# Second attention of a two-block transformer kernel: the outputs of a pair of heads are issued one pair later than its scores and exponentials, and the stage's buffers are cut into smaller parts

## The chip, the core and the metric

The kernel runs on one NeuronCore of a Trainium2 chip. The metric is the device time of one execution in microseconds (us), the median of several runs. Engines: TensorE (PE in the rows; its weight loads are PEld), VectorE (DVE), ScalarE (ACT), GpSimd (POOL) and SyncE (SP, which here issues the DMAs). Each engine works through its own queue in order; semaphores tie the queues together.

## What is computed

All in float32; one sequence of 2048 positions, width 1024. A first block (a short-convolution mixer, then stick-breaking attention) is followed by a second block:

```
proj = h @ w_in                     # u_pool, g_pool, q, k, v, g_attn, qi, ki, wi
pool_out = pool_mixer(u_pool, w_pool) * silu(g_pool)   # means over 2, 4, 8, 16 positions
# attention, for each block of 128 queries, 8 heads that share 2 key heads:
score  = sum over 8 index heads of relu(qi . ki) * wi      # causal
sel    = top 256 keys of score, per query
p      = softmax(q . k over the keys in sel)
attn   = (p @ v) * silu(g_attn)
x      = x + gate * (concat(pool_out, attn) @ w_out)
```

## The kernel before, in words

Activations lie channels by positions, weights are split into a high and a low part, and a projection (`lin`) is three matmuls of 128x512 for each 128 rows of the contraction (L119 to L121 in `lin`). Every phase is a Python generator; `merge` interleaves two or three of them by weights, which gives the order of emission, and a scheduler then sets the final order of each engine's queue from that order, from priorities and from its own model of durations. So the order around the change is the scheduler's, and has to be looked up, not read from the source.

The part that matters here begins after the first attention:

- `phase_e2` makes the gates and the pooling of the second block: `lin`, then on DVE a chain of shifted additions into tiles `ws` (L820), a last scaling (L824), the split into high and low (`split`, L81 on ACT and L82 on DVE, tile `pp`), and in `finish` a matmul of `pp` with `w_pool` (`lin<-pp`).
- `phase_f` is the second attention in eight groups of two query blocks. In step i, three generators are merged: attention of group i (`f_attn`), the search for the selected keys of group i+1 (`f_search`, on DVE: counts at L972, on ACT by a sign at L974, the last values at L1017 and L1018, equal scores at L1038 to L1041, whose result are the `masks`), and the index scores of group i+2 (`f_score`: matmuls L874 and L875, relu on ACT at L877, sum on DVE at L884).
- `f_block` does the attention of one query block, for four pairs of heads. For each head: scores of up to 2048 keys in chunks of 512 (two matmuls, L1150 and L1151, into a PSUM tile `z`), masking and maximum on DVE (L1152, into the row `fe`), the largest maximum (L1159), the bias (L1163), one exponential over the whole row on ACT with its sum (L1164). Then the outputs of the same pair: transposes of `fe` (L1173), copies to SBUF on ACT (L1175), matmuls with the values into `o` (L1181). After four pairs: the reciprocal of the sums, a copy on POOL that spreads it (L1193), four matmuls that turn it (L1197), two multiplications (L1198, L1199) and a store.
- `phase_g` projects with `w_out` for a quarter of the positions; quarters 0 to 2 fill gaps of `phase_f`, quarter 3 comes last.

PSUM has two banks for `z`, shared by index scores and attention scores, two for the transposes `tp`, one for `o` and three for `lin`. The row tiles `fe` are four of up to 2048 elements, so two pairs.

Of the kernel before, what the change touches and what calls it, by code (L numbers as in the profile page):

```python
# [19 lines left out]
P = 128  # L20
# [48 lines left out]
class Build:  # L69
# [72 lines left out]
    def bcast(self, r, name, chunk=None):  # L142

        nc = self.nc
        rb = self.norm_tile(name)
        for c in range(HT // CH) if chunk is None else [chunk]:
            ps = self.bank()
            for i in range(CH // P):
                b = c * (CH // P) + i
                nc.tensor.matmul(  # L150
                    ps[:, i * P : (i + 1) * P], r[:, b : b + 1].to_broadcast([P, P]), self.ident, start=True, stop=True
                )
            nc.scalar.copy(rb[:, c * CH : (c + 1) * CH], ps)
        return rb if chunk is None else rb[:, chunk * CH : (chunk + 1) * CH]
# [42 lines left out]
    def setup(self):  # L197
        nc = self.nc
        self.fixed = self.cp.tile([P, 2 * CH + 4 * CH + 1960], F32, name="fixed")
        self.fixedr = self.cp.tile([P, (4 + 1) * D], F32R, name="fixedr")  # L200
# [50 lines left out]
        own = self.fixedr[:, 4 * D :].rearrange("p (s k m) -> p s k m", s=2, k=4)  # L251
        self.wp = self.load_w("w_pool", 4, 0, own=own, keep=False)
# [523 lines left out]
    def phase_e2(self, chunks, x):  # L776
# [19 lines left out]
        def finish(g, q, ph, pw, sg):  # L796
            pm = self.lin([[w[g]] for w in self.wp], ([ph], [pw]), 1, 0)
# [3 lines left out]
        late = None  # L801
        for g in range(4):
# [31 lines left out]
    def act_chunk(self, pool):  # L834
        t = [pool.tile([P, 2, CH], F32R, name=f"gx{k}", tag="gx", bufs=12) for k in range(NKB)]
# [285 lines left out]
    def f_attn(self, qbs):  # L1121
        for qb in qbs:
            yield from self.f_block(qb)

    def f_block(self, qb):
# [5 lines left out]
        sg = self.turn("fsg", 1)  # L1131
        self.dma(sg.rearrange("p (j n) -> p j n", j=4), self.sg2[h][:, :, qs])
        o = self.psum("o")
        den = self.small("den", 8)
        for p in range(4):
            kv = p // 2
            q = self.turn("fq", 2)
            for d in range(2):
                self.dma(q[d * 64 : (d + 1) * 64], self.q2s[h][:, 2 * p : 2 * p + 2, :, qs])
            pe = []  # L1140
            for a in range(2):
                hd = 2 * p + a
                mx = self.small("mx", 4)
                row = self.at.tile([P, -(-W // HT) * HT], F32, name="fe", tag="fe", bufs=4)
                for c in range(nch):
                    c0 = c * CH
                    m = min(CH, W - c0)
                    keys = self.k2t[c0 // HT][:, kv, c0 % HT : c0 % HT + m]
                    z = self.psum("z")
                    nc.tensor.matmul(z[:, :m], q[:, a, 0], keys, start=True, stop=False)  # L1150
                    nc.tensor.matmul(z[:, :m], q[:, a, 1], keys, start=False, stop=True)  # L1151
                    nc.vector.tensor_tensor_reduce(  # L1152
                        row[:, c0 : c0 + m], z[:, :m], mb[:, c0 : c0 + m], 1.0, NEG, ALU.subtract, ALU.max, mx[:, c : c + 1]
                    )
                    yield 0.43 * m / CH
                sc = self.rq[:, qb, hd : hd + 1]
                if nch > 1:
                    top = self.small("ftop", 1)
                    nc.vector.tensor_reduce(top, mx[:, :nch], mybir.AxisListType.X, ALU.max)  # L1159
                else:  # L1160
                    top = mx[:, 0:1]
                nbs = self.small("nbs", 1)
                nc.vector.scalar_tensor_tensor(nbs, top, -1.0, sc, ALU.mult, ALU.mult)  # L1163
                nc.scalar.activation(row[:, :W], row[:, :W], AF.Exp, bias=nbs, scale=sc, accum_out=den[:, hd : hd + 1])  # L1164
                pe.append(row)
            for c in range(nch):
                nb = min(4, qb + 1 - 4 * c)
                wts = []
                for a in range(2):
                    tp = self.psum("tp")  # L1170
                    for j in range(nb):
                        k0 = c * CH + j * P
                        nc.tensor.transpose(tp[:, j * P : (j + 1) * P], pe[a][:, k0 : k0 + P], self.ident)  # L1173
                    wt = self.turn("fwt", 3)
                    last = nc.scalar.copy(wt[:, : nb * P], tp[:, : nb * P])  # L1175
                    wts.append(wt)
                with self.burst(last) as first:
                    for j in range(nb):
                        for a in range(2):
                            first(  # L1180
                                nc.tensor.matmul(  # L1181
                                    o[a * 64 : (a + 1) * 64, p * P : (p + 1) * P],
                                    self.v2t[c // 2][:, 4 * (c % 2) + j, kv * 64 : (kv + 1) * 64],
# [263 lines left out]
```

## Time and profile before

| | |
|---|---|
| median of 3 runs | 3415.56 us (3414.56 to 3417.75) |
| the profiled execution's own time | 3404.53 us, its span 3402.8 us |
| mean granted clock of TensorE | 0.973 of full speed |
| busy in the span | PE 3193.5 us, DVE 2254.1, ACT 1482.5, POOL 488.1 |

The profiled execution is 11 us below the median of the timed runs; durations and waits come from it alone. A line of the engines' busy times is an average over stages with different limits: the second attention, which the change touches, lies between about 2100 and 3400 us, and its own rows are read by stretch.

### The profile page before, as it was taken

How to read it: one execution, taken by the hardware profiler on the slowest of the kernel's cores; microseconds unless marked ns; L12 is line 12 of the kernel's file. 1: busy time of each engine (PE TensorE's matmuls, PEld its weight loads, DVE VectorE, ACT ScalarE, POOL GpSimd, SP SyncE). 2: the span in 40 equal slices, each digit the busy share in tenths (PEclk: the TensorE clock that was granted, in tenths of full speed). 3: DMA queues.
4: the chain of work that ended last, by engine and by line, in shares of the span. 5: the costliest groups of instructions: out<-in, count | busy, mean ns of one | idle time of the engine just before them, and what ended most of it. 6: DMA issues, size and time to landing. Idle time of an engine off the chain costs nothing. (4 is left out here: it accounts for less than half of the span.)

```text
span 3402.8 us, 49280 instructions
## 1 busy us (share of the span) xinstructions
PE 3193.5 (94%) x17922; PEld 2544.7 (75%) x17922; DVE 2254.1 (66%) x4508; ACT 1482.5 (44%) x2666; POOL 488.1 (14%) x600
## 2 busy tenths in 40 slices
PE   8999999999999999988999998889996998879897
PEld 7888888888788777766788776668875776657675
DVE  5344644544444987789888687998648578888641
ACT  4111411122222544556555555563453465865561
POOL 0000010000200000052212113420200431102002
PEclk9999999999999999999999999899998999999999
DMA  3111442333454554574466444645522552124005
GB/s 107 47 50 50 152 158 80 131 113 128 143 164 146 155 156 143 164 236 115 140 188 178 140 129 132 200 150 171 180 90 99 173 174 78 45 69 155 25 27 178
DMA packets 371396, 438.72 MB, mean 129 GB/s; under 512 B 25664, under 2 KB 271936, under 8 KB 371136
## 3 DMA queue, kind: packets, MB, share of 16 engines
q1 hardware_dynamic: 371136, 435.39, 41.3%
q8 instruction: 146, 2.39, 0.3%
q14 instruction: 114, 0.93, 0.1%
HBM read 308.94 MB, written 124.78 MB: 127 GB/s over the span
## 5 line engine op out<-in xcount | busy, mean ns | idle before, releaser
L119 PE MATMUL lin<-act,fixedr 128*128 128x512 f32 x1488 | 598.0, 402 | 12.7 <-DVE x1r L599 6.2
L120 PE MATMUL lin<-act,fixedr 128*128 128x512 f32 x1488 | 596.0, 401 | 7.1 <-DVE act L620 5.2
L121 PE MATMUL lin<-act,fixedr 128*128 128x512 f32 x1488 | 593.0, 399 | 0.0
L104 ACT ACTIVATE fixedr<-fixed 128x512 fp32r<-128x512 f32 x295 | 186.7, 634 | 729.8 <-PE lin L120 259.7
L548 DVE TENSOR_TENSOR_SCAN crf<-crf 128x512 f32<-128x512 f32 (+3 forms) x320 | 360.2, 1132 | 73.7 <-ACT crf L545 71.1
L119 PEld LDWEIGHTS lin<-act,fixedr 128*128 128x128 f32 x1488 | 283.2, 190 | 78.5 <-DVE x1r L599 8.4
L120 PEld LDWEIGHTS lin<-act,fixedr 128*128 128x128 f32 x1488 | 282.4, 190 | 72.1 <-DVE act L620 8.9
L105 DVE TENSOR_TENSOR fixedr<-fixed,fixedr 128x512 fp32r<-128x512 f32 x295 | 202.1, 685 | 198.5 <-ACT fixedr L104 189.1
L121 PEld LDWEIGHTS lin<-act,fixedr 128*128 128x128 f32 x1488 | 282.3, 190 | 62.1 <-issue 0.2
L1152 DVE CUSTOM_DVE_ANT_0 fe<-z,masks 128x512 f32<-128x512 f32 (+3 forms) x320 | 187.0, 606 | 131.9 <-PE z L1151 74.2
L119 PE MATMUL z<-act,fixedr 128*128 128x512 f32 x584 | 231.0, 396 | 12.0 <-ACT fixedr L104 12.0
L557 ACT COPY crf<-tp 128x512 f32<-128x512 f32 (+3 forms) x320 | 165.1, 530 | 175.9 <-PE tp L555 156.9
L551 POOL TENSOR_TENSOR crf<-crf 128x1 f32<-128x1 f32 x192 | 96.4, 504 | 931.9 <-ACT crf L538 672.6
L121 PE MATMUL z<-act,fixedr 128*128 128x512 f32 x584 | 229.8, 394 | 0.0
L120 PE MATMUL z<-act,fixedr 128*128 128x512 f32 x584 | 229.7, 394 | 0.0
L1175 ACT COPY ff<-tp 128x512 f32<-128x512 f32 (+3 forms) x320 | 160.0, 521 | 152.4 <-PE tp L1173 76.1
L538 ACT ACTIVATE crf<-z 128x512 f32<-128x512 f32 (+3 forms) x320 | 175.4, 549 | 112.8 <-PE tp L555 83.1
L884 DVE SCALAR_TENSOR_TENSOR sc<-ff,fixed,sc 128x512 f32<-128x512 f32 (+3 forms) x266 | 179.2, 694 | 53.1 <-ACT ff L877 51.3
L1173 PE MATMUL tp<-fixed,fe 128*128 128x128 f32 x1088 | 182.9, 287 | 31.7 <-ACT fe L1164 28.9
L1164 ACT ACTIVATE fe<-fe,fixed 128x128 f32<-128x128 f32 (+15 forms) x128 | 165.8, 1295 | 98.3 <-DVE fixed L1163 97.8
L549 DVE TENSOR_TENSOR crf<-crf 128x511 f32<-128x511 f32 (+3 forms) x320 | 198.3, 624 | 10.5 <-DVE crf L548 0.5
L877 ACT ACTIVATE ff<-z 128x512 f32<-128x512 f32 (+3 forms) x304 | 157.7, 544 | 99.0 <-PE z L875 94.0
(343 smaller groups left out, 6527.8 us busy)
## 6 DMA issues: line engine op xcount, KB each, us to landing
fixed<-in_w_in_a_dram SPq DMA_DIRECT2D x128, 256.0 KB, 2.8
fixedr<-kept_w_out SPq DMA_DIRECT2D x64, 512.0 KB, 4.8
kept_w_in<-fixedr SPq DMA_DIRECT2D x46, 512.0 KB, 4.2
fixedr<-kept_w_in SPq DMA_DIRECT2D x46, 512.0 KB, 3.5
crr<-kst SPq DMA_DIRECT2D x80, 256.0 KB, 5.1
crr<-qst SPq DMA_DIRECT2D x64, 256.0 KB, 5.7
fixed<-x2d SPq DMA_DIRECT2D x64, 256.0 KB, 3.8
ffr<-q2s SPq DMA_DIRECT2D x128, 128.0 KB, 2.7
```

Of the source, the lines that this page charges most:

```text
L104: nc.scalar.activation(t[:, 0], raw, AF.Copy)
L105: nc.vector.tensor_tensor(t[:, 1], raw, t[:, 0].bitcast(F32), ALU.subtract)
L119: self.nc.tensor.matmul(ps[:, :n], whi[k], a, start=k == 0, stop=False)
L120: self.nc.tensor.matmul(ps[:, :n], whi[k], b, start=False, stop=False)
L121: self.nc.tensor.matmul(ps[:, :n], wlo[k], a, start=False, stop=k == nk - 1)
L538: nc.scalar.activation(s[:, :W], z[:, :W], AF.Sigmoid)
L548: nc.vector.tensor_tensor_scan(er, er, er, left, ALU.mult, ALU.min)
L549: nc.vector.tensor_tensor(s[:, : W - 1], s[:, : W - 1], e[:, 1:W], ALU.mult)
L884: nc.vector.scalar_tensor_tensor(sc[:, c0 : c0 + m], r[:, :m], w, sc[:, c0 : c0 + m], ALU.mult, ALU.add)
L1152: nc.vector.tensor_tensor_reduce(row[:, c0 : c0 + m], z[:, :m], mb[:, c0 : c0 + m], 1.0, NEG, ALU.subtract, ALU.max, mx[:, c : c + 1])
L1164: nc.scalar.activation(row[:, :W], row[:, :W], AF.Exp, bias=nbs, scale=sc, accum_out=den[:, hd : hd + 1])
L1173: nc.tensor.transpose(tp[:, j * P : (j + 1) * P], pe[a][:, k0 : k0 + P], self.ident)
```

## The change

`f_block` is divided. `f_weights` does scores, masking and exponentials of one pair; `f_outputs` does transposes, copies and output matmuls. `f_attn` calls `f_outputs` for the pair before (kept in `self.behind`), also across blocks and groups; the last group empties it. The rows `fe` become eight tiles of 1024 (the same memory), and an exponential is done for each 1024 keys, so blocks 8 to 15 have two exponentials and two partial sums per head. The reciprocal is no longer spread by POOL: eight matmuls with 64 columns of weights read it through a stride of zero. The activations' tiles are halves of the former ones, the tiles `gx` of `phase_g` are 8 in place of 12, the `w_pool` weights are loaded by `phase_e2` in place of the start, and two merging weights differ.

```
-    def f_attn(self, qbs):
+    def f_attn(self, qbs, last):
         for qb in qbs:
-            yield from self.f_block(qb)
+            self.outs[qb] = [None, None]
+            for p in range(4):
+                pe = yield from self.f_weights(qb, p)
+                if self.behind is not None:
+                    yield from self.f_outputs(*self.behind)
+                self.behind = qb, p, pe
+        if last:
+            yield from self.f_outputs(*self.behind)
+            self.behind = None
...
-                row = self.at.tile([P, -(-W // HT) * HT], F32, name="fe", tag="fe", bufs=4)
+            row = [self.at.tile([P, HT], F32, name="fe", tag="fe", bufs=8) for _ in range(0, W, HT)]
...
-                nc.scalar.activation(row[:, :W], row[:, :W], AF.Exp, bias=nbs, scale=sc, accum_out=den[:, hd : hd + 1])
+            for u, x in enumerate(row):
+                x = x[:, : min(HT, W - u * HT)]
+                nc.scalar.activation(x, x, AF.Exp, bias=nbs, scale=sc, accum_out=den[:, u, hd : hd + 1])
...
-        rr = self.turn("frr", 1)
-        nc.gpsimd.tensor_copy(rr.rearrange("p (a d) -> p a d", a=8), rd.unsqueeze(2).to_broadcast([P, 8, 64]))
-        bc = self.psum("z")
-        for p in range(4):
-            ps = slice(p * P, (p + 1) * P)
-            nc.tensor.matmul(bc[:, ps], rr[:, ps], self.ident, start=True, stop=True)
+            bc = self.psum("z")
+            for i in range(4):
+                ps = slice(i * P, (i + 1) * P)
+                for a in range(2):
+                    row = rd[:, 2 * i + a : 2 * i + a + 1].to_broadcast([P, 64])
+                    nc.tensor.matmul(bc[a * 64 : (a + 1) * 64, ps], row, self.ident, start=True, stop=True)
...
-        t = [pool.tile([P, 2, HT], F32R, name=f"act{i}", tag=f"{pool.name}x", bufs=8) for i in range(n)]
-        return [x[:, 0] for x in t], [x[:, 1] for x in t]
+        t = [pool.tile([P, HT], F32R, name=f"act{i}", tag=f"{pool.name}x", bufs=16) for i in range(2 * n)]
+        return t[::2], t[1::2]
...
-        t = [pool.tile([P, 2, CH], F32R, name=f"gx{k}", tag="gx", bufs=12) for k in range(NKB)]
+        t = [pool.tile([P, 2, CH], F32R, name=f"gx{k}", tag="gx", bufs=8) for k in range(NKB)]
...
-        self.wp = self.load_w("w_pool", 4, 0, own=own, keep=False)
...
+        wp = self.load_w("w_pool", 4, 0, own=self.wk.tile([P, 2, 4, P], F32R, name="wp", tag="wp", bufs=1))
...
-            merge((self.ahead(self.phase_c(1), 2000), 250), (de, 300))
+            merge((self.ahead(self.phase_c(1), 2000), 260), (de, 300))
...
-            merge((de, 300), (until(f, lambda: self.e2), 230))
+            merge((de, 300), (until(f, lambda: self.e2), 250))
```

Three places of the queues show what the scheduler made of it.

**DVE, end of the pooling against the selection of blocks 8 and 9.** Before, the last additions `ws` of one chunk (L820, L824, L82) stand between and behind the selection's last steps (L1038 to L1041, `masks`):

```order
L1039 SCALAR_TENSOR_TENSOR masks_15956<-masks_15956 128x1152
L1032 COPY_PREDICATED fixed_84<-fixed_84 128x2
L1040 SCALAR_TENSOR_TENSOR masks_15956<-masks_15956,fixed_84 128x1152
L1041 SCALAR_TENSOR_TENSOR masks_15956,fixed_84<-sc_18628,fixed_84,masks_15956 128x1152
L820 TENSOR_TENSOR ws_20194<-ws_20192 128x525
L1038 TENSOR_SCALAR masks_15956<-sc_18629,fixed_84 128x1280
L82 TENSOR_TENSOR gx1_20295<-fixed_84,gx1_20295 128x512
L820 TENSOR_TENSOR ws_20196<-ws_20194 128x521
L1039 SCALAR_TENSOR_TENSOR masks_15956<-masks_15956 128x1280
L820 TENSOR_TENSOR ws_20198<-ws_20196 128x513
```

After, the same chunk (L819, L823 there) stands among the steps of the search itself, which are short but for the counts (L971); the steps on equal scores (L1037 to L1040 there) come some 70 rows later:

```order
L819 TENSOR_TENSOR ws_20244<-ws_20242 128x525
L977 SCALAR_TENSOR_TENSOR fixed_84<-fixed_84 128x4
L984 SCALAR_TENSOR_TENSOR fixed_84<-fixed_84 128x2
L819 TENSOR_TENSOR ws_20246<-ws_20244 128x521
L979 COPY_PREDICATED fixed_84<-fixed_84 128x8
L986 RECIPROCAL fixed_84<-fixed_84 128x2
L819 TENSOR_TENSOR ws_20248<-ws_20246 128x513
L991 TENSOR_TENSOR fixed_84<-fixed_84 128x2
L987 TENSOR_TENSOR fixed_84<-fixed_84 128x2
L823 SCALAR_TENSOR_TENSOR ws_20248<-ws_20248,u_20180 128x512
```

So the pooling's chain no longer has the selection's long last steps ahead of it.

**PE, the last pair of block 8.** Before, the last scores of the pair's second head (`z_22174`) are followed after 22 instructions by the first transpose of that head's row (`fe_22165`):

```order
L1151 MATMUL z_22174<-keys_18565,ffr_15958 128x128
L874 MATMUL z_22201<-keys_18565,ffr_15958 128x256
L875 MATMUL z_22201<-keys_18565,ffr_15958 128x256
L1173 MATMUL tp_22105<-fixed_84,fe_21978 128x128
L1181 MATMUL o_21552<-ff_15957,keys_15903 64x128 x8
L1173 MATMUL tp_22181<-fixed_84,fe_22144 128x128 x4
L874 MATMUL z_22208<-keys_15903,ffr_15958 128x512
L875 MATMUL z_22208<-keys_15903,ffr_15958 128x512
L1181 MATMUL o_21552<-ff_15957,keys_18565 64x128 x2
L874 MATMUL z_22281<-keys_15903,ffr_15958 128x512
L875 MATMUL z_22281<-keys_15903,ffr_15958 128x512
L1173 MATMUL tp_22187<-fixed_84,fe_22165 128x128
```

After, the same scores (`z_22176`) stand here, with outputs of the pair before and projections of `phase_g` (`lin<-gx`) behind them:

```order
L1161 MATMUL z_22176<-keys_18619,ffr_16025 128x128
L1221 MATMUL o_21871<-ff_16024,keys_18619 64x128 x2
L1213 MATMUL tp_22229<-fixed_84,fe_22007 128x128 x4
L120 MATMUL lin_22317<-gx3_21758,fixedr_85 128x512
L873 MATMUL z_22180<-keys_18619,ffr_16025 128x256
L874 MATMUL z_22180<-keys_18619,ffr_16025 128x256
L121 MATMUL lin_22317<-gx3_21758,fixedr_85 128x512
```

and the first transpose of that head's row (`fe_22166`) stands here, 101 instructions behind those scores:

```order
L1161 MATMUL z_22367<-keys_15966,ffr_16025 128x512
L121 MATMUL lin_22460<-gx7_21762,fixedr_85 128x512
L119 MATMUL lin_22567<-gx0_21755,fixedr_85 128x512
L120 MATMUL lin_22567<-gx0_21755,fixedr_85 128x512
L121 MATMUL lin_22567<-gx0_21755,fixedr_85 128x512
L119 MATMUL lin_22567<-gx1_21756,fixedr_85 128x512
L1221 MATMUL o_21871<-ff_16024,keys_18619 64x128 x2
L1213 MATMUL tp_22400<-fixed_84,fe_22166 128x128 x4
```

What moved: the way from a row's scores to its transposes on PE is over four times as many instructions long here. In blocks 13 to 15, where scores of the next pair already stood ahead of outputs before, it grows less.

**PE, from block 9 to block 10.** Before, the last outputs of block 9 (`o_22311`) come ahead of 16 pairs of index scores and then the first scores of block 10; the end of that piece:

```order
L875 MATMUL z_23024<-keys_18565,ffr_15958 128x512
L874 MATMUL z_23029<-keys_18565,ffr_15958 128x256
L875 MATMUL z_23029<-keys_18565,ffr_15958 128x256
L1150 MATMUL z_23060<-keys_15903,ffr_15958 128x512
L1151 MATMUL z_23060<-keys_15903,ffr_15958 128x512
```

After, block 10's first two rows of scores (`z_23133` to `z_23185`) stand ahead of the normalizer (L1204) and of the last pair's transposes of block 9 (L1213):

```order
L1160 MATMUL z_23176<-keys_15966,ffr_16025 128x512
L1161 MATMUL z_23176<-keys_15966,ffr_16025 128x512
L873 MATMUL z_23180<-keys_15966,ffr_16025 128x512
L874 MATMUL z_23180<-keys_15966,ffr_16025 128x512
L1160 MATMUL z_23185<-keys_18619,ffr_16025 128x384
L1161 MATMUL z_23185<-keys_18619,ffr_16025 128x384
L1204 MATMUL z_23193<-fixed_84 64x128 x8
L873 MATMUL z_23223<-keys_18619,ffr_16025 128x512
L874 MATMUL z_23223<-keys_18619,ffr_16025 128x512
L873 MATMUL z_23248<-keys_18619,ffr_16025 128x384
L874 MATMUL z_23248<-keys_18619,ffr_16025 128x384
L1213 MATMUL tp_23339<-fixed_84,fe_23131 128x128 x4
```

So a block's last outputs now lie behind scores that need the next group's masks on DVE.

## Rows read from the trace of the kernel before

**Rows 1.** The page's first part: busy us, share of the span, instructions.

```profile
PE 3193.5 (94%) x17922; PEld 2544.7 (75%) x17922; DVE 2254.1 (66%) x4508; ACT 1482.5 (44%) x2666; POOL 488.1 (14%) x600
```

**Rows 2.** Windows: busy us by engine, granted clock, DMA share, GB/s.

```profile
2580.00:2611.00 31.00, 28.82 (x128) 22.96 (x126) 24.85 (x101) 14.72 (x21) 2.10 (x7) 1.00 0.43 147
2611.00:2640.00 29.00, 1.95 (x6) 1.29 (x5) 28.02 (x62) 4.83 (x10) 3.49 (x3) 0.52 0.03 9
2640.00:2783.00 143.00, 137.08 (x801) 108.07 (x800) 83.22 (x190) 72.43 (x131) 44.78 (x46) 0.95 0.53 170
2783.00:3177.00 394.00, 341.04 (x2262) 265.28 (x2262) 350.44 (x987) 239.01 (x404) 82.40 (x71) 0.95 0.28 90
2783.00:2864.00 81.00, 73.04 (x439) 57.86 (x439) 77.31 (x226) 42.89 (x74) 33.17 (x24) 0.96 0.39 127
2931.00:3037.00 106.00, 88.02 (x625) 66.11 (x624) 100.16 (x295) 77.44 (x124) 8.20 (x7) 0.93 0.12 33
3088.00:3177.00 89.00, 75.39 (x522) 59.58 (x521) 86.02 (x248) 44.32 (x65) 15.82 (x10) 0.95 0.28 95
3177.00:3332.00 155.00, 145.09 (x1259) 109.93 (x1258) 61.58 (x220) 95.71 (x142) 2.22 (x5) 0.99 0.08 23
```

**Rows 3.** Timeline of PE at 2638 us: start, us, instruction, idle before.

```profile
2638.42 0.79 PE L119 MATMUL lin<-pp,fixedr 128*128 128x512 f32 x1 [27.05 <-ACT pp L81]
2639.01 0.63 PE L119 MATMUL lin<-act,fixedr 128*128 128x512 f32 x1
...
2642.85 0.47 PE L119 MATMUL lin<-act,fixedr 128*128 128x512 f32 x1
...
2645.26 0.40 PE L120 MATMUL lin<-act,fixedr 128*128 128x512 f32 x1
```

**Rows 4.** Timeline of DVE in the same stretch.

```profile
2629.61 0.70 DVE L820 TENSOR_TENSOR ws<-ws 128x525 f32<-128x525 f32 x1
...
2632.24 2.81 DVE L1039 TENSOR_TENSOR_SCAN masks<-masks 128x1280 int16<-128x1280 int16 x1
...
2637.02 0.68 DVE L824 SCALAR_TENSOR_TENSOR ws<-ws,u 128x512 f32<-128x512 f32 x1
```

**Rows 5.** Waits of PE from 2783 to 3177: us in total, times, longest.

```profile
PE tp L1173 <- ACT fe L1164: 21.5, 9, 6.5
PE z L1150 <- DVE fixed L1152: 10.9, 5, 3.8
PE o L1181 <- ACT ff L1175: 6.6, 6, 2.0
...
PE z L1197 <- POOL ff L1193: 1.8, 2, 1.3
```

**Rows 6.** Timeline of all engines around 2855 us.

```profile
2854.10 1.68 DVE L1041 SCALAR_TENSOR_TENSOR masks<-sc,fixed,masks 128x1408 uint8<-128x1408 f32 x1
...
2855.70 0.15 DVE L1163 SCALAR_TENSOR_TENSOR fixed<-fixed 128x1 f32<-128x1 f32 x1
...
2857.38 0.90 PE L1173 MATMUL tp<-fixed,fe 128*128 128x128 f32 x3 [6.46 <-ACT fe L1164]
```

**Rows 7.** Groups by shape: busy us, mean ns of one.

```profile
L1164 ACT ACTIVATION_READ_ACCUMULATOR fe<-fe,fixed 128x1 f32 x128 | 24.2, 189 | 0.0
L1164 ACT ACTIVATE fe<-fe,fixed 128x2048 f32<-128x2048 f32 x8 | 16.8, 2099 | 5.2 <-DVE fixed L1163 5.2
L1164 ACT ACTIVATE fe<-fe,fixed 128x1024 f32<-128x1024 f32 x8 | 9.9, 1244 | 1.0 <-DVE fixed L1163 0.9
```

**Rows 8.** Timeline of PE in the last block.

```profile
3317.12 1.09 PE L1181 MATMUL o<-ff,keys 128*64 128x128 f32 x16 [1.48 <-ACT ff L1175]
...
3318.64 1.06 PE L1197 MATMUL z<-fixed,ff 128*128 128x128 f32 x8
```

**Rows 9.** Timeline of all engines around 2609 us.

```profile
2608.62 1.13 ACT L1164 ACTIVATE fe<-fe,fixed 128x896 f32<-128x896 f32 x1
...
2611.23 0.15 DVE L975 TENSOR_SCALAR fixed<-fixed 128x1 f32<-128x1 f32 x1 [2.45 <-ACT masks L974]
```

More of the change, by code (lines that the diff above doesn't have):

```diff
@@ L140, in rstd, with bcast @@
         return r
-    def bcast(self, r, name, chunk=None):
+    def bcast(self, r, name, chunk=None, into=None):
         nc = self.nc
-        rb = self.norm_tile(name)
+        rb = self.norm_tile(name) if into is None else into
         for c in range(HT // CH) if chunk is None else [chunk]:
@@ L1130, in f_block @@
         mb = self.masks[qb]
[L1131 to L1134, printed above, removed]
-        for p in range(4):
[L1136 to L1140, printed above, removed]
-            for a in range(2):
-                hd = 2 * p + a
-                mx = self.small("mx", 4)
-                row = self.at.tile([P, -(-W // HT) * HT], F32, name="fe", tag="fe", bufs=4)
[L1145 to L1163, printed above, removed]
-                nc.scalar.activation(row[:, :W], row[:, :W], AF.Exp, bias=nbs, scale=sc, accum_out=den[:, hd : hd + 1])
[L1165 to L1183, printed above, removed]
-                                    wts[a][:, j * P : (j + 1) * P],
-                                    start=(c == 0 and j == 0),
-                                    stop=(c == nch - 1 and j == nb - 1),
-                                )
-                            )
-                yield 0.44 * nb
@@ new lines, in f_weights, with f_outputs @@
+        if p == 3:
+            rd = self.small("rd", 8)
+            if W > HT:
+                nc.vector.tensor_tensor(rd, den[:, 0], den[:, 1], ALU.add)
+                nc.vector.reciprocal(rd, rd)
+            else:
+                nc.vector.reciprocal(rd, den[:, 0])
+            self.outs[qb][1] = rd
+        return pe
+    def f_outputs(self, qb, p, pe):
+        nc = self.nc
+        h, qs = qb // 8, slice(qb % 8 * P, qb % 8 * P + P)
+        nch = (qb * P + P + CH - 1) // CH
+        kv = p // 2
+        sg = self.gates[qb]
+        if p == 0:
+            self.outs[qb][0] = self.psum("o")
+        o, rd = self.outs[qb]
+        if p == 3:
+            bc = self.psum("z")
+            for i in range(4):
+                ps = slice(i * P, (i + 1) * P)
+                for a in range(2):
+                    row = rd[:, 2 * i + a : 2 * i + a + 1].to_broadcast([P, 64])
+                    nc.tensor.matmul(bc[a * 64 : (a + 1) * 64, ps], row, self.ident, start=True, stop=True)
+            nc.vector.tensor_tensor(sg, bc, sg, ALU.mult)
+        for c in range(nch):
+            nb = min(4, qb + 1 - 4 * c)
+            wts = []
+            for a in range(2):
+                tp = self.psum("tp")
+                for j in range(nb):
+                    k0 = c * CH + j * P
+                    nc.tensor.transpose(tp[:, j * P : (j + 1) * P], pe[a][k0 // HT][:, k0 % HT : k0 % HT + P], self.ident)
+                wt = self.turn("fwt", 3)
+                last = nc.scalar.copy(wt[:, : nb * P], tp[:, : nb * P])
+                wts.append(wt)
+            with self.burst(last) as first:
+                for j in range(nb):
+                    for a in range(2):
+                        first(
+                            nc.tensor.matmul(
+                                o[a * 64 : (a + 1) * 64, p * P : (p + 1) * P],
+                                self.v2t[c // 2][:, 4 * (c % 2) + j, kv * 64 : (kv + 1) * 64],
+                                wts[a][:, j * P : (j + 1) * P],
+                                start=(c == 0 and j == 0),
+                                stop=(c == nch - 1 and j == nb - 1),
+                            )
+                        )
+            yield 0.44 * nb
+        if p == 3:
+            nc.vector.tensor_tensor(sg, o, sg, ALU.mult)
+            self.dma(self.cata[h][:, :, qs], sg.rearrange("p (j n) -> p j n", j=4))
+            self.seen[qb] = self.small("seen", 1)
+            nc.gpsimd.tensor_copy(self.seen[qb], sg[:, 0:1])
+            self.attended += 1
+            yield 1.0
@@ L1230, in phase_f @@
             )
+        self.behind, self.outs, self.den, self.gates = None, {}, {}, {}
         for i in range(-2, len(groups)):
```

64 lines of the change are left out of this document (43 added, 21 removed).

## The prediction, made before the changed kernel ran

> **What bounds the kernel now.** I read the page's first part, then the second attention cut into windows, then PE's waits in the worst of these, then the timelines around the two largest. PE is busy 3193.5 of 3402.8 us [rows 1], so 209 us are all that could come back at unchanged PE work, and the change touches only waits that lie in the second attention. The windows [rows 2] show three kinds of stretch there. From 2611 to 2640 us PE does almost nothing (1.95 of 29 us) while DVE works 28.02: a hole with DVE as its cause. From 2783 to 3177 us PE works 341.0 and DVE 350.4 of 394: neither is full over the whole of it; in the three selections inside it (2783 to 2864, 2931 to 3037, 3088 to 3177) DVE has 263.5 of 276 us, so DVE bounds these, and PE bounds what lies between. From 3177 to 3332 us PE is at 145.1 of 155 and DVE at 61.6: PE bounds the last blocks. From 2640 to 2783 likewise (137.1 of 143).
>
> The hole is one wait of 27.05 us of the pooling's matmul for its input `pp` [rows 3]. DVE's timeline says why [rows 4]: the pooling's additions (L820, L824) stand among the selection's last steps for blocks 8 and 9, of which the scan L1039 alone takes 2.81 us. After the hole the first nine matmuls come at (2642.85 - 2639.01) / 9 = 0.427 us each, the next ten at (2645.26 - 2642.85) / 10 = 0.241 [rows 3]; the granted clock of the hole's window is 0.52 [rows 2], so the idle stretch also cost clock, of the two levels the one of 1.2 GHz.
>
> In the stretch from 2783 to 3177 us PE waits 21.5 us for exponentials, 10.9 for DVE to free a bank of scores, 6.6 for copies, 1.8 for the normalizer's copy on POOL [rows 5]. The longest of them, 6.46 us, is a chain in which ACT was not late by itself: DVE did L1041 of the selection for 1.68 us, then at 2855.70 the bias L1163, only then could ACT start, and PE's transposes came at 2857.38 [rows 6].
>
> **What the change does to each.**
>
> *The hole.* After the change the chunk's additions stand among the short search steps, ahead of the steps on equal scores. The wait of 27.05 us goes, and with it the slow matmuls, 9 x (0.427 - 0.241) = 1.7 us. What is late next: `pp` still needs its chain through DVE, whose search steps contain counts. I leave +6 us for the last chunks' small waits; the bounds are 0 (every chunk hidden behind its two projections of 24 matmuls, 48 x 0.241 = 11.6 us) and 27 (the wait only changes its place). I choose near the low end because in the order none of the 2 to 3 us steps stands inside the chain any more. Sum: -27.05 - 1.7 + 6 = -22.8.
>
> *The lag.* The transposes of a row come more than a hundred instructions after its scores where they came after 22, so the 6.46 us and its like should be covered. But a wait of PE that goes returns time only where DVE can also go on: in the selections DVE is idle 276 - 263.5 = 12.5 us, in the whole stretch 394 - 350.4 = 43.6. The bounds are therefore 0 and about -44 (the waits of [rows 5] add up to 40.8). I take -10, near the 12.5: the exponential waits lie mostly where DVE is full. From 3177 on, PE already runs nearly without gaps, so I count nothing there.
>
> *The normalizer.* POOL's copy goes, and with it PE's waits of 1.8 us [rows 5]. Four matmuls of 128 columns of weights become eight of 64. The old four take 1.06 us (8 records), and eight matmuls of the very new shape, the outputs, take 1.09 (16 records) [rows 8]: so 16 blocks x 0.03 = 0.5 us, nothing. Sum -1.8 + 0.5 = -1.3. The Trainium skill, "TensorE: Matmul & The Clock Gate", section "Back-to-back issue gap", prices a matmul by its moving columns alone; by that, eight with 128 moving columns would take twice the four, 1.06 x 16 = 17 us more. The trace's 1.09 against 1.06 us speaks against it here, where consecutive matmuls go to the two halves of the output partitions.
>
> *The split exponentials.* Blocks 8 to 15 have 64 rows wider than 1024, so 64 exponentials more. Two of 1024 and the extra read cost 2 x 1244 + 189 - 2099 = 578 ns more than one of 2048 [rows 7], 64 x 0.578 = 37 us of ACT. ACT is busy 239 of 394 and 95.7 of 155 us there [rows 2]; the cover is the lag itself, since PE does another pair's outputs meanwhile. If that cover is gone, a pair pays up to 0.58 us for each head. The Trainium skill, "VectorE: DVE Perf Modes", section "The TRN2 errata — SBUF-src ops pay a fixed extra latency per instruction", speaks against such splitting: small tiles pay the fixed part each. With its 224 cycles of ScalarE the estimate is 64 x 0.19 = 12 us; the rows here give three times that, since the read of the sum is paid as well.
>
> *The rest.* Loading `w_pool` in `phase_e2` adds one load, one split and one store for the first half and a load for the second, where the DMA engines are at 0.43 and less [rows 2]: 0. Halved activation tiles keep their bytes: 0. With eight `gx` tiles in place of twelve a quarter of `phase_g` can't load ahead; quarters 0 to 2 are filling, so 0, at worst some 5 us where a quarter follows directly. The merging weights move the beginnings of phases by little in the order: 0.
>
> *Sum:* -22.8 - 10 - 1.3 = -34.1 us against the profiled execution's 3404.5, which gives 3370.4, a ratio of 0.9900. The runs' median is 3415.56, so 3381.
>
> **The rivals.**
>
> 1. *Slower: ACT delays the search.* One of a selection's two counts runs on ACT (L974), and DVE waits for it at each of its eight steps; at 2611.23 DVE waited 2.45 us because an exponential of 1.13 us stood ahead [rows 9]. Now two heads' exponentials stand together, so a count may find a second row ahead of it: 2 x 1244 + 2 x 189 ns = 2.9 us. With three selections from 2783 on, 24 steps: at 2.0 us each DVE, already full, is 48 us longer; -22.8 - 1.3 + 48 = +24, 3439. It decides from 24 / 24 = 1.0 us a step on; from (24 + 7) / 24 = 1.3 it is slower by more than measurement can tell. Against it: ACT is busy 239 of 394 us only, and the scheduler can put the count first.
> 2. *Only the hole closes.* DVE sets the pace of the selections, and PE's waits for exponentials turn into waits for DVE's masks or for a bank of scores, since block 10's scores now stand ahead of block 9's last outputs. Then -22.8 - 1.3: 3380.4 profiled, 3391.5.
> 3. *The change doesn't do what it says:* the hole moves to a neighbouring chunk (the +6 becomes 27) and the lag returns only a few us: -2 to -8, some 3410.
> 4. *Everything comes back:* hole without a rest and all of DVE's idle time: -28.8 - 43.6 - 1.3 = -73.7, which is 3342. In favour: the clock of 0.95 in that stretch [rows 2] would rise with fewer gaps.
> 5. *The eight matmuls cost double,* as the skill's rule has it: 3381 + 17 = 3398. The mechanism in this kernel would be that the two halves don't overlap when the weights are read through a stride of zero.
>
> **How the numbers follow.** The forecast has a chance of 0.44 (3381, its own range 3366 to 3393), rival 2 0.18, rival 1 0.17, rival 4 0.10, rival 5 0.05, rival 3 0.06. A measurement of this kernel tells about 0.2%, 6.8 us, from no change, so the border is 3408.7. Of the four cases that gain, 0.77 together, I move 0.06 across it, for the uncertainty of a sum of this kind; so faster 0.71. Rival 1 spills 0.01 into the middle and keeps 0.16, and 0.02 of rival 3 turns slower: 0.18. The same: the rest, 0.11. The range for 8 in 10 runs from 3350 (leaving out half of rival 4) to 3428 (leaving out the greater part of rival 1): about 0.05 below and 0.13 above.
>
> **What the profile after would show.** Hole right: no PE wait above about 3 us for `pp`, and DVE's steps on equal scores behind the pooling's last split. Lag right: PE's waits for exponentials between the first selection and the last below 5 us in place of 21.5, and the stretch from block 10's selection to the last one shorter than 394 us. Lag useless: the same sum of PE waits there under another name (scores for DVE). ACT right: exponentials 192 in number, ACT's busy time some 37 us up, and DVE's waits for L974's counterpart not above the 2.45 us a step seen here. Normalizer: sixteen records in about 1.1 us. The prediction is wrong above all if DVE's selections get longer, or if a new wait of 20 us appears at another boundary of phases, since the scheduler reorders every queue.

## The result, and the profile after

The changed kernel takes 3372.81 us (median of 4 runs, 3368.09 to 3374.52) against 3415.91 us before (4 runs, 3414.56 to 3417.75): a ratio of 0.9871, 95% interval 0.9854 to 0.9888, or 43 us less. The forecast was 3381 with a range from 3350 to 3428. The profiled execution's span fell from 3402.8 to 3366.0 us.

The first part of the page after, which answers to [rows 1]:

```profile
PE 3213.1 (95%) x18050; PEld 2546.6 (76%) x18050; DVE 2244.8 (67%) x4516; ACT 1502.8 (45%) x2794; POOL 464.9 (14%) x584
```

PE's idle time went from 3402.8 - 3193.5 = 209.3 us to 3366.0 - 3213.1 = 152.9, 56.4 us less; but its busy time rose by 19.6 us, which the forecast did not have. The difference is the 36.8 us of the span.

The windows of the changed kernel, with the columns of [rows 2]: from just behind the pooling's end to the selection of blocks 10 and 11; from there to the end of the last selection; the three selections; the last blocks:

```profile
2640.00:2760.00 120.00, 114.36 (x722) 88.26 (x723) 77.27 (x178) 62.22 (x117) 31.26 (x25) 0.99 0.42 134
2760.00:3146.00 386.00, 352.39 (x2308) 265.52 (x2309) 350.54 (x990) 255.70 (x492) 73.34 (x73) 0.96 0.34 107
2760.00:2858.00 98.00, 96.69 (x589) 75.06 (x589) 91.79 (x265) 58.07 (x117) 33.47 (x32) 0.98 0.56 179
2909.00:3031.00 122.00, 107.17 (x775) 77.94 (x774) 114.25 (x319) 97.13 (x185) 9.20 (x7) 0.98 0.13 38
3041.00:3146.00 105.00, 96.46 (x593) 73.65 (x593) 95.73 (x262) 55.89 (x95) 23.79 (x25) 0.97 0.49 156
3146.00:3301.00 155.00, 148.06 (x1304) 110.88 (x1300) 64.84 (x228) 103.29 (x185) 0.79 (x5) 1.00 0.09 27
```

Against [rows 2] the stretch of the selections is 386 us long in place of 394, with the same DVE work (350.5 and 350.4) but 352.4 us of PE work in place of 341.0: PE's idle time in it fell from 53.0 to 33.6. Each selection by itself got longer (81 to 98, 106 to 122, 89 to 105 us), because more of DVE's other work now lies inside it: in the second, for example, 14 us more of the sums of index scores (L883). By the prediction that was the first sign of its being wrong; it came, and the kernel is faster all the same.

PE's longest waits in that stretch, which answer to [rows 5]:

```profile
PE z L1160 <- DVE fixed L1162: 7.2, 5, 1.8
PE z L1160 <- ACT ff L876: 6.3, 8, 2.1
PE z L873 <- ACT ff L876: 5.8, 5, 3.6
PE tp L1213 <- ACT fe L1176: 5.2, 6, 1.9
```

The wait for exponentials fell from 21.5 to 5.2 us. In its place stand waits of 12.1 us for a PSUM bank that ACT's relu (L876) has yet to read (in L1160 and L873): PE runs ahead of ACT and DVE now, where before it stood behind them.

The hole, on PE and then on DVE, answering to [rows 3] and [rows 4]:

```profile
2627.86 0.51 PE L119 MATMUL lin<-pp,wp 128*128 128x512 f32 x1 [3.14 <-ACT pp L81]
```

```profile
2624.63 0.68 DVE L823 SCALAR_TENSOR_TENSOR ws<-ws,u 128x512 f32<-128x512 f32 x1
...
2636.03 2.56 DVE L1038 TENSOR_TENSOR_SCAN masks<-masks 128x1152 int16<-128x1152 int16 x1
```

27.05 us became 3.14: the last scaling of the pooling (L823) now comes 11 us ahead of the first long step on equal scores (L1038).

### The profile page after: what moved, and what is told of

Same layout as the page of the kernel before. It is cut to its first block, busy times and chain, and to the rows that moved or that the text cites. A ratio compares the mean times of both kernels' runs of the same rounds, so it can differ in the third digit from the quotient of the medians.

```text
span 3366.0 us, 49652 instructions
## 1 busy us (share of the span) xinstructions
PE 3213.1 (95%) x18050; PEld 2546.6 (76%) x18050; DVE 2244.8 (67%) x4516; ACT 1502.8 (45%) x2794; POOL 464.9 (14%) x584
## 5 line engine op out<-in xcount | busy, mean ns | idle before, releaser
L1176 ACT ACTIVATE fe<-fe,fixed 128x1024 f32<-128x1024 f32 (+7 forms) x192 | 189.5, 991 | 74.2 <-DVE fixed L1173 73.6
L883 DVE SCALAR_TENSOR_TENSOR sc<-ff,fixed,sc 128x512 f32<-128x512 f32 (+3 forms) x266 | 177.7, 692 | 47.8 <-ACT ff L876 47.2
L1213 PE MATMUL tp<-fixed,fe 128*128 128x128 f32 x1088 | 189.8, 284 | 16.4 <-ACT fe L1176 11.5
L876 ACT ACTIVATE ff<-z 128x512 f32<-128x512 f32 (+3 forms) x304 | 156.9, 547 | 92.4 <-PE z L874 72.9
```

Source lines behind the costliest of these rows:

```text
L883: nc.vector.scalar_tensor_tensor(sc[:, c0 : c0 + m], r[:, :m], w, sc[:, c0 : c0 + m], ALU.mult, ALU.add)
L1176: nc.scalar.activation(x, x, AF.Exp, bias=nbs, scale=sc, accum_out=den[:, u, hd : hd + 1])
L1213: nc.tensor.transpose(tp[:, j * P : (j + 1) * P], pe[a][k0 // HT][:, k0 % HT : k0 % HT + P], self.ident)
```

## The experiments

Besides the parts told ahead, the change loads a block's gate with its second pair, keeps `phase_g`'s broadcast in the buffer that POOL's copy had, takes the reciprocal right behind the last exponentials and counts finished blocks one by one.

Not every part could be taken back by itself: SBUF has no room for most such kernels. It has room for one with the second set of activation tiles whole; that is the base (e1) of most others, and they are compared with it.

**e1: the second set of activation tiles whole.**

```
+        if pool.name == "xb":
+            t = [pool.tile([P, 2, HT], F32R, name=f"act{i}", tag=f"{pool.name}x", bufs=8) for i in range(n)]
+            return [x[:, 0] for x in t], [x[:, 1] for x in t]
...
-            pool(name="xb", bufs=16) as xb,
+            pool(name="xb", bufs=8) as xb,
```

> The changed kernel with one part undone: the second set of activation tiles is whole again (8 tiles with both halves) instead of 16 halves; it serves as the base of the next runs, which don't fit the memory otherwise. All theories: the order on DVE at the end of the pooling is that of the changed kernel, so within 0.2% of it, 3366 to 3380 us. If the halving of the tiles were a part of the gain, it would be slower by 5 us or more.

3368.51 us, ratio 0.9851 (0.9838 to 0.9863). The same as the changed kernel within the intervals: halving these tiles gives nothing by itself.

**e2: no lag.** Base e1 and

```
-                if self.behind is not None:
-                    yield from self.f_outputs(*self.behind)
-                self.behind = qb, p, pe
-        if last:
-            yield from self.f_outputs(*self.behind)
-            self.behind = None
+                yield from self.f_outputs(qb, p, pe)
...
-        if p == 1:
+        if p == 0:
             sg = self.gates[qb] = self.turn("fsg", 1)
```

> As the run before it, but the outputs of a pair follow its own scores at once (no lag). Main theory (two separate gains, the hole by the merging weight and the lag by its cover): no hole at the pooling, PE's waits for exponentials between the selections back to about 20 us, 8 to 14 us slower than the base, 3381 to 3390. Rival A (the lag closes the hole too): the wait of 27 us for pp is back, 3400 or more. Rival B (the lag gives nothing, since DVE bounds the selections): within 5 us of the base.

3395.28 us, 0.9941 (0.9927 to 0.9954): 26.8 us over e1, more than twice what the main theory gave. No wait for `pp` is among PE's waits, so rival A falls, and rival B too. The stretch of the selections in e1, its window and the longest of PE's waits in it by exponentials, DVE, copies and weight loads (its two longest are by relu):

```profile
2766.00:3155.00 389.00, 358.77 (x2381) 269.81 (x2379) 353.91 (x1006) 260.33 (x501) 73.69 (x74) 0.97 0.34 108
```

```profile
PE lin L119 <- DMA fixedr<-kept_w_out: 4.7, 4, 2.5
PE tp L1216 <- ACT fe L1179: 4.5, 5, 1.9
PE o L1224 <- ACT ff L1218: 3.5, 4, 1.4
PE z L1163 <- DVE fixed L1165: 2.5, 2, 1.5
```

and in e2:

```profile
2776.00:3184.00 408.00, 353.79 (x2397) 270.61 (x2396) 355.59 (x1013) 263.96 (x505) 78.94 (x66) 0.96 0.28 89
```

```profile
PE tp L1211 <- ACT fe L1174: 15.9, 10, 4.4
PE lin L119 <- DMA fixedr<-kept_w_out: 8.8, 1, 8.8
PE z L1158 <- DVE fixed L1160: 6.5, 8, 1.7
PE o L1219 <- ACT ff L1213: 6.5, 7, 3.0
...
PE z L1202 <- DVE fixed L1180: 3.4, 3, 1.9
```

DVE has nearly the same work (353.9 and 355.6 us), PE idles 54 us in place of 30. Of these 24 us the waits for exponentials are 11.4; a weight load that comes late by 8.8 us adds 4.1, and whether the lag or another turn of the order has to do with that is not shown. The last row is new against [rows 5]: without the lag the new normalizer (L1202) waits for the reciprocal (L1180), since nothing stands between them any more.

**e3: the merging weight back to 230.** Base e1 and

```
-            merge((de, 300), (until(f, lambda: self.e2), 250))
+            merge((de, 300), (until(f, lambda: self.e2), 230))
```

> As the base run, with the lag, but the merging weight of the second attention against the projections is 230 as before. Main theory: the selection's steps on equal scores stand ahead of the last pooling additions again, PE waits 20 to 27 us there, and the time is 18 to 25 us over the base, 3390 to 3400. Rival A (the lag closes the hole): within 5 us of the base, no wait for pp above 5 us.

3400.47 us, 0.9951 (0.9938 to 0.9964): 32.0 us over e1, where 18 to 25 were expected. The hole is back, with the lag in place:

```profile
PE lin L119 <- ACT pp L81: 23.1, 1, 23.1
```

against 3.5 us in e1. So with everything else as in e1 the weight decides the hole, and the lag doesn't close it. The span is 3399.6 us against 3369.1, and PE idles 188.4 us of it against 162.5: of the 30.5 us the wait itself is 23.1 - 3.5 = 19.6, other idle time 6.3 and busy time 4.6, at a mean granted clock of 0.974 in place of 0.978.

**e4: the two weights alone, in the kernel before.**

```
-            merge((self.ahead(self.phase_c(1), 2000), 250), (de, 300))
+            merge((self.ahead(self.phase_c(1), 2000), 260), (de, 300))
...
-            merge((de, 300), (until(f, lambda: self.e2), 230))
+            merge((de, 300), (until(f, lambda: self.e2), 250))
```

> The kernel before with nothing changed but the two merging weights (260 and 250). If the weight alone closes the hole, 3390 to 3397 us. If the weight needs the other parts of the change (the order there still has the steps on equal scores ahead of the last additions), 3408 to 3420 and the wait for pp of 20 to 27 us stays.

3406.68 us, 0.9981 (0.9972 to 0.999): 9 us less by the medians, and the wait stays:

```profile
PE lin L119 <- ACT pp L81: 20.2, 1, 20.2
```

The weight closes the hole only together with another part of the change; e5 below says more on which.

**e8 and e11: the attention of the kernel before, all else changed.** Base e2, and whole rows (e7's edit below), and

```
+            rr = self.turn("frr", 1)
+            nc.gpsimd.tensor_copy(rr.rearrange("p (a d) -> p a d", a=8), rd.unsqueeze(2).to_broadcast([P, 8, 64]))
             bc = self.psum("z")
             for i in range(4):
                 ps = slice(i * P, (i + 1) * P)
-                for a in range(2):
-                    row = rd[:, 2 * i + a : 2 * i + a + 1].to_broadcast([P, 64])
-                    nc.tensor.matmul(bc[a * 64 : (a + 1) * 64, ps], row, self.ident, start=True, stop=True)
+                nc.tensor.matmul(bc[:, ps], rr[:, ps], self.ident, start=True, stop=True)
```

and in e11 also

```
-        rb = self.bcast(self.rd[:, h, :8], "rbg", q % 2, None if self.exact else self.turn("rbg", 1))
+        rb = self.bcast(self.rd[:, h, :8], "rbg", q % 2, None)
```

In e8 two uses share one buffer, so its output has other scales; the instructions are the same.

> e1 without the lag, with whole rows and with the old normalizer (copy on POOL, four matmuls): only the tiles, the loading of w_pool and the merging weights are those of the changed kernel. If the rest closes the hole without the lag: no wait above 5 us for pp and 3385 to 3398 us. If the lag or the halved rows were needed for the hole, 3405 or more.

> As e8 (no lag, whole rows, old normalizer with POOL's copy), with a buffer of its own for the broadcast in phase_g, where e8 shared one with the normalizer's copy and so had other scales in its output. If that sharing cost nothing, 3393 to 3403 us as e8; if it cost waits, 3385 to 3393. In both cases no wait above 5 us for pp.

3401.03 us, 0.9958 (0.9943 to 0.9972), and 3402.69 us, 0.9964 (0.9952 to 0.9977); e8 lies just above its expectation's upper end, e11 at the edge of the first of its two cases. The wait for `pp` in e8 and in e11:

```profile
PE lin L119 <- ACT pp L81: 1.5, 1, 1.5
```

```profile
PE lin L119 <- ACT pp L81: 1.8, 1, 1.8
```

So neither the lag nor the halved rows nor the new normalizer is needed to close it; but without the lag all the rest, the closed hole in it, is worth 12 to 13.5 us against the kernel before, half of its 27.05. e2, which differs from e11 in the split rows, the new normalizer and the buffer of `phase_g`'s broadcast, is 7 us faster; which of them does that was not taken apart. Sharing the buffer costs nothing that can be told.

**e12: the fourth corner,** e2 with e3's weight.

> The fourth corner: e1 without the lag (as e2) and with the weight of 230 (as e3). Lag with the hole closed was worth 26.8 us (e2 against e1), the hole with the lag 32.0 (e3 against e1). If the two simply add up, 3400.5 + 26.8 = 3427. If the hole's gain is partly lost without the lag, because the selection's last steps then fall into the attention behind it where PE waits for DVE, the lag is worth less with the hole open: 3408 to 3418, with a wait of 20 to 27 us for pp and about 20 us less DVE work between the end of the pooling and the next selection than in e2.

3439.90 us, 1.0065 (1.0052 to 1.0079): above both cases, and slower than the kernel before.

```profile
PE lin L119 <- ACT pp L81: 28.0, 1, 28.0
PE tp L1211 <- ACT fe L1174: 24.7, 14, 5.6
...
PE z L1158 <- DVE fixed L1160: 13.7, 15, 2.0
...
PE z L1202 <- DVE fixed L1180: 7.4, 7, 1.9
```

| us | weight 250 | weight 230 | the weight |
|---|---|---|---|
| lag | 3368.5 (e1) | 3400.5 (e3) | 32.0 |
| no lag | 3395.3 (e2) | 3439.9 (e12) | 44.6 |
| the lag | 26.8 | 39.4 | |

Each of the two is worth more while the other is missing, and the rest of the change, without both, costs 24 us (3439.9 against 3415.9).

**e7 and e9: whole rows with the lag.** e7 is the changed kernel with

```
-            row = [self.at.tile([P, HT], F32, name="fe", tag="fe", bufs=8) for _ in range(0, W, HT)]
+            row = self.at.tile([P, -(-W // HT) * HT], F32, name="fe", tag="fe", bufs=4)
...
-            for u, x in enumerate(row):
-                x = x[:, : min(HT, W - u * HT)]
-                nc.scalar.activation(x, x, AF.Exp, bias=nbs, scale=sc, accum_out=den[:, u, hd : hd + 1])
+            nc.scalar.activation(row[:, :W], row[:, :W], AF.Exp, bias=nbs, scale=sc, accum_out=den[:, 0, hd : hd + 1])
...
```

and e9 is the same on the base of e1.

> The changed kernel, lag included, but the rows are whole again (four of up to 2048, one exponential and one sum for each). My price of the split was 37 us of ACT, hidden: so PE's waits for exponentials change by less than 5 us and the time is within 0.3% of the changed kernel, 3363 to 3383. If the smaller parts help (a transpose can begin after the first half), it is slower by over 0.3%; if ACT was loaded by them, it is faster by as much.

> The changed kernel with its lag, new normalizer and weights, but with whole rows (one exponential each, as in e7) and a whole second set of activation tiles (as in e1). e1 was 3368.5 and e7 3373.7 us in calls of their own. If halving does nothing, within 0.2% of e1, 3362 to 3375. If each whole part saves a little (37 us less work for ACT, in e7 the shortest stretch of selections, 373 us), 3355 to 3362, the best of all.

3373.72 us, 0.9878 (0.9862 to 0.9893), and 3366.35 us, 0.9857 (0.9839 to 0.9875). Both within the intervals of their partners (0.9871 and 0.9851): the smaller rows neither help nor cost.

**e10: the normalizer's matmuls twice,** on the base of e1.

```
                     nc.tensor.matmul(bc[a * 64 : (a + 1) * 64, ps], row, self.ident, start=True, stop=True)
+                    nc.tensor.matmul(bc[a * 64 : (a + 1) * 64, ps], row, self.ident, start=True, stop=True)
```

> As e1, but the eight matmuls of the normalizer are issued twice (the second time over the same bank, the result is the same), 128 matmuls more in all. My prediction's price is 1.09 us for eight, so +17 us of PE work; the trace of the changed kernel shows 18.8 us for all of them, against 13.8 for the old four. If PE is full around the blocks' ends, 12 to 20 us above e1. If DVE sets the pace there, less than 6 us above it.

3380.49 us, 0.9898 (0.9883 to 0.9913): 12.0 us over e1 by the medians, 0.75 us for each block's eight matmuls, the lower end of the first case. By the ratios, since the two were measured at different times, it is 16 us, 1.0 us each. PE's busy time is 3218.6 us against 3206.6 in e1, 12.0 more.

**e5 and e6: where the weights lie.** The profile after had shown something that no line of the diff names: in `phase_a`, which the change doesn't touch but for its tiles, PE is full in both kernels but does fewer matmuls per time, and later it is the other way round. e5 is e1 with

```
-        self.fixedr = self.cp.tile([P, 4 * D], F32R, name="fixedr")
+        self.fixedr = self.cp.tile([P, 5 * D], F32R, name="fixedr")
```

which makes the allocator place the weights at byte 77952 of a partition, as before, and not at 98080. e6 gives `phase_a` a ring of weights of its own at byte 16512:

```
+            kept = self.rings["weights"]
+            wa = self.at.tile([P, 4 * D], F32R, name="wa", tag="wa", bufs=1)
+            self.rings["weights"] = wa.rearrange("p (n s k m) -> p n s k m", n=4, s=2, k=4)
             run(self.phase_a(0, xa, xb))
             merge((self.phase_a(1, xa, xb), 420), (self.adaln(), 9))
+            self.rings["weights"] = kept
```

> As e1, but the tile that holds the weights is 4 KB larger (unused), which makes the allocator swap it with the tile of small buffers: the weights lie at byte 77952 of a partition, as in the kernel before, and not at 98080, as in the changed kernel. What the traces show so far: a 128x512 matmul of a projection follows the one before it after 0.227 us where weights and moving activations lie on the same side of about 98304, and after 0.232 to 0.234 us where they lie on different sides; in the kernel before phase_a (activations low) is fast and the later phases slow, in the changed kernel the other way round. If the place is the cause: phase_a ends at 913 to 916 us in place of 924, the later projections take 0.234 in place of 0.227 us, and the time is 5 to 15 us above e1. If the pitch belongs to the run or to the other engines' traffic, it stays as in e1 and the time is within 5 us of e1.

> As e1, but phase_a uses a ring of weights of its own at byte 16512 of a partition, on the side of 11 of its 16 tiles of activations; the later phases keep the ring at 98080, on the side of theirs. If the place is the cause: about 11/16 of phase_a's matmuls at 0.227 us, phase_a some 8 to 12 us shorter than in e1, and the whole 3355 to 3362 us. If not, within 4 us of e1.

e5: 3403.54 us, 0.9962 (0.9947 to 0.9976); e6: 3371.19 us, 0.9865 (0.9845 to 0.9884). Windows in `phase_a` and in a later run of projections, all at full granted clock and with PE never idle. The kernel before:

```profile
100.00:200.00 100.00, 100.00 (x441) 82.42 (x440) 41.20 (x54) 18.22 (x27) 1.16 (x2) 1.00 0.18 53
1030.00:1080.00 50.00, 50.00 (x215) 40.21 (x214) 17.90 (x28) 11.79 (x19) 0.00 (x0) 1.00 0.57 176
```

the changed kernel:

```profile
100.00:200.00 100.00, 100.00 (x430) 80.42 (x429) 39.88 (x53) 17.74 (x26) 1.16 (x2) 1.00 0.17 51
1030.00:1080.00 50.00, 50.00 (x224) 41.40 (x223) 18.98 (x29) 11.62 (x19) 0.00 (x0) 1.00 0.62 189
```

and e5:

```profile
100.00:200.00 100.00, 100.00 (x440) 82.42 (x439) 39.93 (x52) 17.54 (x26) 1.16 (x2) 1.00 0.18 50
1030.00:1080.00 50.00, 50.00 (x215) 40.21 (x214) 18.40 (x28) 11.00 (x19) 0.00 (x0) 1.00 0.56 174
```

The numbers of matmuls (behind PE's busy time) follow the place of the weights: 441 and 440 against 430 in `phase_a`, 215 and 215 against 224 later. `phase_a` ends at 913.5 us in e5, at 924.4 in e1, as the first case said. The whole time of e5, 35 us above e1 where 5 to 15 were expected, is no measure of the place: its order differs in the second attention, and the hole is open again there:

```profile
PE lin L119 <- ACT pp L81: 22.3, 1, 22.3
```

That bears on the hole. e5 has the lag and the weight of 250; what it lacks against e1 is 4 KB of a partition for the other tiles, which the change had freed by loading `w_pool` late, and the place of the weights. So the weight of 250 doesn't suffice there either. What goes with the hole in all fourteen kernels is the order on DVE: in the five that wait 20 us or more for `pp` (the kernel before, e3, e4, e5, e12) both scans over equal scores of blocks 8 and 9 start ahead of at least the last two scalings of the pooling, in e5 at 2623.1 and 2631.3 us with scalings at 2634.0, 2642.1 and 2655.0; in the nine others all scalings come first, in e1 the last at 2629.3 and the scans at 2641.4 and 2656.2.

e6 gained 2.6 us in `phase_a` (its end at 921.8) where 8 to 12 were expected, and nothing in the whole, which is its second case. In part that is because tiles found no room on the low side and went to the other: by the allocation, 58% of the matmuls of the first 900 us have weights and activations on one side, where e1 has 24% and e5 78%. In proportion `phase_a` would end near 918 us, an estimate from e1 and e5; the other 4 us are open.

## Why the prediction was right, point by point

**The bound** was read rightly in the main: of the 56.4 us of PE's idle time that went, 43 lay in the hole and in the stretch of the selections. Another 8 lay behind it, from 3177 us on in the kernel before, where the prediction counted nothing.

**The hole,** -22.8: the mechanism is shown. Scans ahead of the pooling's last scalings go with the wait in every kernel, and their order is what the prediction named; e2, e8 and e11 show that the lag has no part in it. The size is too small: 32.0 us with the lag (e3). The wait itself gave 24 (27.05 to 3.14) and the rest I had left (+6) was 3. What I had not counted is what goes with it elsewhere: by e3 another 6.3 us of PE's idle time and 4.6 of its busy time. I had taken the order as it stood, without asking which part makes it, and had put the merging weights at 0: by e3 and e12 the weight brings the hole back and is worth 32.0 and 44.6 us. It isn't enough by itself: in the kernel before it leaves 20.2 us (e4), and in e5 22.3. By e8 and e11 the other part it needs is among the tiles, the loading of `w_pool`, the earlier reciprocal and the count of finished blocks; e5 points at the room that the late loading frees or at the place of the weights, and which of these two acts is open.

**The lag,** -10: it covers the exponentials as predicted (PE waits 4.5 us for them in e1, 15.9 in e2), but its price is the step that failed in size: 26.8 us (e2) and 39.4 (e12). I had said that a wait of PE that goes returns time only where DVE can also go on, and had bounded what could return by DVE's 12.5 idle microseconds inside the selections. That is wrong as a bound of the gain: a selection need not get shorter. In e1 and e2, which differ in the lag, the three selections (from a group's first count to its last step on equal scores) take 326 us with the lag and 289 without, and what lies between them 63 and 119. Other work moved into the selections, they got longer, and what lay between them got shorter by more. The other bound, all of DVE's idle time in the whole stretch (43.6), is one that the measured gains keep.

**The normalizer,** -1.3: the price was somewhat low. PE's busy time for it, as a group by shape shows, in the kernel before and in the changed one:

```profile
L1197 PE MATMUL z<-fixed,ff 128*128 128x128 f32 x128 | 20.3, 283 | 1.8 <-POOL ff L1193 1.8
```

```profile
L1204 PE MATMUL z<-fixed 128*64 128x128 f32 x256 | 20.9, 288 | 1.7 <-DVE fixed L1162 1.7
```

Such a sum counts each matmul to its own end, although the next one starts before that. Counted from each start to the next, it is 13.8 us before and 18.8 after: 5.0 us more in place of 0.5. e10 prices eight of them at 0.75 to 1.0 us, where twice the old four would be 2.1. So rival 5, the rule of the Trainium skill ("TensorE: Matmul & The Clock Gate", section "Back-to-back issue gap") whose figures go by the moving columns, so that twice the matmuls with the same moving columns take twice as long, doesn't hold for these pairs on two halves of the output: 18.8 is 1.36 times 13.8. What I had not seen is that without the lag this form waits for the reciprocal, 7.4 us in e12, where POOL's copy had cost 1.8.

**The split exponentials,** 37 us of ACT and hidden: hidden is right, 37 is too much. The groups of the changed kernel, exponentials and reads of their sums:

```profile
L1176 ACT ACTIVATE fe<-fe,fixed 128x1024 f32<-128x1024 f32 (+7 forms) x192 | 189.5, 991 | 74.2 <-DVE fixed L1173 73.6
...
L1176 ACT ACTIVATION_READ_ACCUMULATOR fe<-fe,fixed 128x1 f32 x192 | 36.8, 192 | 0.0
```

That is 36.3 us more than the 165.8 and 24.2 of before, but these durations overlap: in one pair of the changed kernel the read begins at 2709.72 us and its exponential ends at 2709.81. ACT's busy time as a whole rose by 20.3 us (1482.5 to 1502.8), and e7, with whole rows and otherwise the changed kernel, has 23.4 us less than that:

```profile
PE 3209.1 (95%) x18050; PEld 2545.0 (76%) x18050; DVE 2239.6 (67%) x4508; ACT 1479.4 (44%) x2666; POOL 462.5 (14%) x584
```

That is 0.37 us for each of the 64 splits in place of 0.578, and e7 and e9 find no time in it. The Trainium skill's fixed part ("VectorE: DVE Perf Modes", section "The TRN2 errata — SBUF-src ops pay a fixed extra latency per instruction"), an estimate of 12 us, is about half of what was measured; the reads, 36.8 us in place of 24.2, are about the other half.

**The rest,** 0: wrong in its parts. The merging weight is worth 32.0 us or more, as said. The place of the weights moved: `phase_a` ends 11.6 us later (926.8 against 915.2), and later projections are faster. And the corner without lag and weight (e12) is 24 us slower than the kernel before. So the sum of -34 (measured: -37 in the profiled execution, -43 by the medians) came near by compensation, which is luck: both gains are larger than I had them, by some 9 and 17 us if each is taken out of e1 by itself (e3, e2), and a loss of the rest that I had at nothing stands against them. Of PE's 19.6 us more busy time the slower `phase_a` gives 13.7 (899.4 us up to its end before, 913.1 after), but the faster projections behind it take 11 back, counted from each start to the next; the normalizer gives 5. What is left, some 12 us in the matmuls of the two attentions, and e12's 24 us are open.

**The rivals.** Rival 1 did not come, though the selections got longer: DVE's waits for ACT's counts fell. In the kernel before and in the changed one, by what DVE waited for at the step behind the count:

```profile
  ACT masks L974: 10.0, 16
```

```profile
  ACT masks L973: 4.9, 8
```

Rival 2 (only the hole) is excluded by e2. Rival 3 is what e4 looks like, the weights without the rest. Rival 4 did not come with its 74 us, but more of PE's idle time went than I had forecast, 56.4 us.

## What to carry to other kernels

When two engines share a stretch in which neither is full, the idle time of the busier one inside its own fullest part is no limit for the gain: a lag lets work from behind fill that part. Judge by the sum over the whole stretch. Where a stage is merged by weights and a scheduler, check each part of a change with the others present: here the weights alone gave 9 us, all but weight and lag a loss of 24, and the whole 43; and 4 KB of unused memory, with the move of the weights that it brought, were enough to open the hole again. Look up the order that came out each time. And compare matmuls per microsecond in stretches where the engine is never idle; a difference there is not a wait and doesn't show among the waits.

## What the runs showed of the hardware

A matmul of 128x512 in float32r, in unbroken runs at the granted clock of 1.00, follows the one before it at one of two mean spacings. In a run of 288 projections that begins near 1030 us it is 0.2342 us in the kernel before (weights from byte 77952 to 94336 of a partition, activations above 118000) and 0.2268 us in the changed kernel (weights from 98080 on, activations above 114000). With the allocation of the built programs beside the traces, the fast time goes with weights and activations on the same side of a border near byte 98000, the slow one with different sides: in the kernel before, some 3500 matmuls at a mean of 0.228 us on one side and some 5400 at 0.234 on two; in the first 900 us of e1, some 890 at 0.229 and 2800 at 0.233. Moving the weights moved `phase_a`'s time (e5). Where exactly the border lies, and why, these runs don't tell: the weights that count as low end at 94336, those that count as high begin at 98080, and no activations lie near. That activations on the high side next to low weights are slow even between fast ones in the same run speaks for the address and against other engines' traffic.
